# A decoder layer whose last stage adds finished tiles to the output in DRAM by DMA

## The chip, the cores and the metric

The kernel runs on one core of a Trainium2 chip. A core has a matrix engine (TensorE, PE in the profile, with PEld for its weight loads), VectorE (DVE), ScalarE (ACT), GpSimd (POOL) and SyncE (SP), which here only issues DMAs. Each engine takes its instructions in order; semaphores hold an instruction until what it needs is done. Matmul results land in PSUM, which has banks of 512 float32 per partition; everything else on chip lies in SBUF. Sixteen DMA engines move data between SBUF and DRAM. SP's DMAs go through the queue that the profile calls q1, GpSimd's through q0; only GpSimd's can add to their destination instead of overwriting it.

The metric is the device time of one execution in microseconds, smaller is better.

## The reference

One decoder layer over a sequence of 1024 tokens with 1024 features, all in float32:

```
x = x + 0.5 * swiglu(rms_norm(x) ; ffn1)            # 1024 -> 2816 -> 1024
h = rms_norm(x) @ w_in                              # q, k, v and gates of two attentions
x = x + (sig(g_fox) * (fox @ w_bf) + sig(g_sb) * (stick @ w_bs)) @ w_out
x = x + 0.5 * swiglu(rms_norm(x) ; ffn2)
x = x + sigmoid(rms_norm(x) @ w_ple_gate) * (p @ w_ple_proj)
```

`fox` is causal softmax attention with forget gates, `stick` is stick-breaking attention. The change touches the first line, small parts of the others, and the last line.

## The kernel before, in words

**Exact products from rounded operands.** TensorE is fed in the faster type float32r. So each operand is split into a high half (a copy rounded to float32r, on ScalarE) and a low half (the rest, a subtraction on VectorE, sometimes on GpSimd); a product is high x high + high x low + low x high. `split` does this for a weight tile, `high` and `low` for the activations. A product over 512 features is 12 matmuls of 128x128 weights by 512 columns.

**Seven products instead of eight.** `make_up` computes a 1024 x 256 block of weights against 1024 x 1024 activations, cut 2 x 2, by a Strassen scheme: block `n` has products `(n, m)`, m = 1 to 7, whose operands are sums of quarters. On the activation side these sums are `B[m]`, made once per stage by the `combo_...` functions on VectorE and ScalarE, quarter by quarter (`j` = 0 to 3). On the weight side `sums`, `third_sum` and `last_sum` form them from the raw tiles, in place. Product `(n, m)` adds into an open PSUM bank: 1, 6, 7, 4 share one (`b`), 5 and 3 another (`d`), 2 has its own (`a`). `evict(n, m, ps)` takes what is finished out of PSUM and combines it in the tiles `E[n]`.

**The order is written by hand.** `up_order` gives the list of products. The loop of `ffn` (and that of `end` in the last stage) does for step s: the product and its `evict`, then `begin(s)`, which issues the pieces of the activation sums that are due, then `prep` of the product four steps on (`LA = 4`), which splits its weights and, at certain products, forms the block's sums or issues the load of block n + 2. Within `ffn` each engine runs in the order of the program (`manual_schedule`); the attention between the two FFNs is placed by a scheduler. Buffers rotate by tag: a load whose tag is full waits until the tile that it replaces has been read, and since SP is in order everything behind it on SP waits too. In the first FFN the raw weights of the up projection lie in the tags KH and KL, where the activations' working tiles lie too.

In the first FFN (`rows` is true there) steps 8 to 12 are (1,3), (3,1), (1,4), (2,4), (3,2). Product (1,4) is the first to read `B[4]`, which `begin` makes in steps 4 to 8: a difference (`combo_d`), then high and low half (`combo_e`, `L651` and `L655`).

**The head.** `first_entry` loads the rows of x, takes their norms (`rows_stat`: a square with a row sum on ScalarE, plus epsilon, to the power of minus one half on GpSimd), multiplies (`rows_mul`, VectorE), turns them by TensorE (`turn`) and splits them (`rows_high`, `rows_low`). `busy` runs idle matmuls at the start. `plain` is the product of block 0, which is not done by the scheme.

**Norms between the stages.** While the last down products of a stage (`make_down`, steps i = 0 to 6 of four tiles t each) still run, `up_step` already takes the next norm: the squares, a sum over partitions by four thin matmuls (`norm_sum`, L194), the root (`norm_pow`: L199 on ScalarE, L200 on GpSimd), and a turn of the result into a row by TensorE (`norm_row`, L206). In i = 5 the sum stands after t = 1 and the row after t = 2. This holds for the entry of the second FFN and of the last stage; the entry of the attention has its own code.

**The last stage** (`ple_start`). The down products of the second FFN leave x in SBUF; `finished` also stores it to DRAM, into `x_end` (`xe`). The stage has four blocks. `E[n][i]` (i = 0, 1) is a tile of 128 x 2 x 512, the sigmoid of the gate for one 128-row part of the output, its halves called h0 and h1. The table `AT` says what happens at the end of each step: `fetch` loads a tile of the projection `p_proj` (or, with `True`, of the residual x) by SP; `finish` multiplies `E` by the projection (L1722) and then either lets GpSimd issue a DMA that adds the residual from `x_end` into the SBUF tile (L1724) or, `late`, adds a fetched residual on VectorE (L1726); `store` writes the tile to the output by SP (L1730). The last product, (3,4), runs in two halves of 256 columns, in one PSUM bank, with a sigmoid (L1784) after each. Steps 10 to 18 are (3,1), (2,4), (3,2), (3,6), (3,5), (3,7), (2,3), (3,3), (3,4).

## Time and profile before

| | us |
|---|---|
| median of 3 runs | 2250.58 (2249.4 to 2251.67) |
| the profiled execution | 2251.57 |
| its span, first to last instruction | 2249.8 |
| busy: TensorE, VectorE, ScalarE, GpSimd | 2215.0, 1513.7, 1004.5, 817.1 |
| mean granted TensorE clock | 0.998 of full |

A row of the timeline reads: start and duration in us, engine, source line, operation, output <- inputs by tile tag, partitions x elements, how many instructions the row joins, and in brackets how long the engine stood idle before the first and what released it. SPq and POOLq rows are DMA issues. Consecutive instructions of one kind are joined, also where they overlap, so starts are the better measure of a pace. A row of the waits reads: engine, tile, line, `<-` what it waited for, then us in total, times, and the longest. A row of windows gives the stretch and its length, busy us and count for PE, PEld, DVE, ACT, POOL, the granted clock, the share of the 16 DMA engines, and GB/s. A DMA queue's row gives packets, MB and its share of the 16 engines in the window asked for; a DMA issue's row the size and the time to landing.

### The profile page before, as it was taken

Reading aid. Unit: us, or ns where it says so; the run is one execution under the profiler, and the core shown is the slowest. Engines: PE = TensorE matmul, PEld = TensorE weight load, DVE = VectorE, ACT = ScalarE, POOL = GpSimd, SP = SyncE. Lnnn points to the kernel's source line nnn. Section 1 sums busy time; section 2 is a strip of 40 time slices with the busy share of each in tenths; the row PEclk is TensorE's granted clock in tenths of the full one; section 3 lists DMA queues with packets and bytes.
Section 4 is the critical chain, followed back from the end, with each engine's and each line's share of the span. In section 5 each row is a group of like instructions: output and inputs, shape, how many; then the busy total and the mean of one; then the engine's idle time right before and its main releaser. Section 6 shows DMA issues by size and latency. Waiting matters only on the chain. (4 is left out here: it accounts for less than half of the span.)

```text
span 2249.8 us, 30560 instructions
## 1 busy us (share of the span) xinstructions
PE 2215.0 (98%) x11226; PEld 1880.4 (84%) x11226; DVE 1513.7 (67%) x2366; ACT 1004.5 (45%) x1805; POOL 817.1 (36%) x787
## 2 busy tenths in 40 slices
PE   9999999999999999999999999999999999999997
PEld 7788888888888899999898888888888888888886
DVE  8755545598888324666678885789655545778887
ACT  6333333433455435555566663255333333434453
POOL 1343534210021336556566664420544353200111
PEclk9999999999999999999999999999999999999999
DMA  3332323394322334333324366741423232655327
GB/s 132 101 129 80 131 80 131 114 345 171 115 94 98 128 108 127 85 104 89 82 57 100 108 206 218 245 155 52 141 85 126 80 132 80 243 206 192 123 84 224
DMA packets 196184, 298.04 MB, mean 132 GB/s; under 512 B 28730, under 2 KB 108858, under 8 KB 196035
## 3 DMA queue, kind: packets, MB, share of 16 engines
q1 hardware_dynamic: 195312, 293.47, 39.4%
q0 software_dynamic: 720, 2.62, 0.6%
q8 instruction: 88, 1.44, 0.3%
q14 instruction: 62, 0.50, 0.1%
q10 hardware_dynamic: 2, 0.00, 0.0%
HBM read 196.14 MB, written 83.13 MB: 124 GB/s over the span
## 5 line engine op out<-in xcount | busy, mean ns | idle before, releaser
L509 PE MATMUL ps<-H,H 128*128 128x512 f32 x2184 | 497.2, 390 | 0.0
L509 PEld LDWEIGHTS ps<-H,H 128*128 128x128 f32 x2184 | 409.7, 188 | 84.7
L619 PE MATMUL ps<-H,WL 128*128 128x512 f32 x1176 | 278.0, 389 | 0.0
L619 PEld LDWEIGHTS ps<-H,WL 128*128 128x128 f32 x1176 | 220.8, 188 | 45.8
L185 POOL TENSOR_TENSOR PT<-PT,PT 128x512 f32<-128x512 f32 x27 | 34.9, 1293 | 400.7 <-ACT PT L182 399.8
L619 PE MATMUL ps<-H,Q 128*128 128x512 f32 x612 | 145.6, 389 | 0.0
L517 DVE SCALAR_TENSOR_TENSOR X<-ps,X 128x512 f32<-128x512 f32 x168 | 110.3, 686 | 47.6 <-PE ps L509 47.3
L619 PE MATMUL ps<-X,WL 128*128 128x512 f32 (+1 forms) x576 | 135.9, 385 | 0.5 <-ACT KH L1784 0.5
L619 PEld LDWEIGHTS ps<-H,Q 128*128 128x128 f32 x612 | 114.9, 188 | 23.8
L619 PE MATMUL ps<-H,PT 128*128 128x512 f32 x528 | 125.8, 390 | 0.0
L619 PEld LDWEIGHTS ps<-X,WL 128*128 128x128 f32 x576 | 106.7, 188 | 22.2 <-ACT KH L1784 0.7
L139 POOL TENSOR_TENSOR WL<-RAW,WH 128x512 fp32r<-128x512 f32 (+1 forms) x84 | 98.4, 1192 | 67.9 <-ACT WH L129 38.7
L1223 DVE TENSOR_TENSOR PT<-ps,PT 128x512 fp32r<-128x512 f32 (+1 forms) x160 | 100.1, 627 | 30.7 <-ACT PT L1217 29.8
L900 PE MATMUL ps<-WH,H 128*128 128x256 f32 x768 | 116.2, 288 | 0.8 <-ACT RN L965 0.8
L619 PEld LDWEIGHTS ps<-H,PT 128*128 128x128 f32 x528 | 99.0, 188 | 20.5
L908 PE MATMUL ps<-H,WH 128*128 128x512 f32 x384 | 115.1, 407 | 0.0
L1241 PE MATMUL ps<-PT,X 128*128 128x256 f32 (+1 forms) x640 | 102.5, 286 | 6.4 <-DVE PT L1223 5.4
L1217 ACT CAST PT<-ps 128x512 fp32r<-128x512 f32 (+1 forms) x160 | 87.0, 549 | 42.2 <-PE ps L1215 40.8
L1241 PEld LDWEIGHTS ps<-PT,X 128*128 128x128 f32 x640 | 90.3, 190 | 17.0 <-DVE PT L1223 10.5
L900 PEld LDWEIGHTS ps<-WH,H 128*128 128x128 f32 x768 | 101.5, 190 | 2.7 <-ACT RN L965 1.2
L412 POOL TENSOR_TENSOR PT<-GF,RN 128x512 f32<-128x512 f32 x20 | 33.6, 1680 | 189.8 <-DVE GF L808 189.8
L1169 POOL TENSOR_TENSOR T<-T,l 128x128 f32<-128x128 f32 (+3 forms) x64 | 73.2, 1147 | 71.9 <-DVE l L1168 69.8
(457 smaller groups left out, 4792.2 us busy)
## 6 DMA issues: line engine op xcount, KB each, us to landing
hidden<-PT SPq DMA_DIRECT2D x40, 512.0 KB, 2.7
WH<-in_ffn_w_gate_dram SPq DMA_DIRECT2D x38, 512.0 KB, 4.8
Q<-hidden SPq DMA_DIRECT2D x24, 512.0 KB, 6.2
hidden<-RN SPq DMA_DIRECT2D x22, 512.0 KB, 2.6
KH<-in_ffn_w_up_dram SPq DMA_DIRECT2D x20, 512.0 KB, 6.2
KL<-in_ffn_w_up_dram SPq DMA_DIRECT2D x20, 512.0 KB, 6.9
T<-in_ffn_w_down_dram SPq DMA_DIRECT2D x20, 512.0 KB, 6.2
GF<-hidden SPq DMA_DIRECT2D x14, 512.0 KB, 8.0
```

What stands on the lines that cost most here:

```text
L139: ins = eng_lo.tensor_sub(lo[part], raw[part], f(hi[part]))
L185: add = lambda eng: eng.tensor_add(N["acc"], N["acc"], d)
L412: eng.tensor_add(s12[:, 0, :], g1[:, 1, :], g2[:, 1, :])
L509: pe(nc.tensor.matmul(groups[g][t][:], wt[:, b, k, t * P:(t + 1) * P], act[:, a, k, :], start=(fresh and n == 0), stop=(i in (6, 1, 4) and ...
L517: nc.vector.scalar_tensor_tensor(xs, groups[g][t][:], scale, xs, ALU.mult, ALU.add)
L619: pe(nc.tensor.matmul(ps[:, cols], hl[:, a, k, :], right(B[m], b, k)[:, cols], start=(first and i == 0), stop=(final and i == 11), skip_gr ...
L900: pe(nc.tensor.matmul(ps[:, :n], hT[t // 4](a, k)[:, (t % 4) * P:(t % 4 + 1) * P], w[k // 4][b][:, k % 4, :n], start=(i == 0), stop=(i == ...
L908: pe(nc.tensor.matmul(ps[:], w[a][:, k, :], hT[half](b, k), start=(i == 0), stop=(i == 23)))
L1169: nc.gpsimd.tensor_mul(T[:, :n], T[:, :n], l[:].broadcast_to([P, n]))
L1217: high = nc.scalar.copy(pt[:, 0, :width], ps[:, :width])
L1223: ins = nc.vector.tensor_sub(pt[:, 1, :width], ps[:, :width], f(pt[:, 0, :width]))
L1241: pe(nc.tensor.matmul(o, lh, r, start=(kpair == c and i == 0), stop=(kpair == 0 and i == 3)))
```

## The change

1. **Last stage.** `xe` is no longer a tensor of its own but a view of the kernel's output: x is stored there at the end of the second FFN, and residuals are fetched from there. A finished tile is added to the output in DRAM: GpSimd's DMA has the output as destination and the SBUF tile as source. `store` goes. Tiles that are late are, as before, added on VectorE and then written. Products (2,3) and (2,4) change places (steps 11 and 16). By DMA now go both tiles of blocks 0 and 1, (2,0), half h1 of (2,1) and h0 of (3,0); late are h0 of (2,1), h1 of (3,0), and (3,1). The fetches are set anew.
2. **First FFN's order.** Steps 9 to 16 become (3,1), (3,2), (1,4), (2,4), (2,3), (3,6), (3,5), (3,7). The preparations of (1,4) and (3,2) keep the order that they had (`ahead`). The sums of block 3 move from the preparation of (3,2) to that of (3,6), GpSimd's `last_sum` with them.
3. **`begin`.** The first `combo_s` goes from step 1 to step 0, `third_sum(2)` from step 3 to step 2, in all three stages of this kind.
4. **Norms.** In i = 5 the sum is taken after t = 0 instead of t = 1.
5. **Head.** The DMA of the norm's gain is issued ahead of the activation that loads the table; epsilon is added by GpSimd for three of the first four row tiles; `F.prep(0, 2)` goes ahead of `rows_stat(N[1], 0)` and `rows_low(N[0], 3)`; `F.prep(2, 1)` goes ahead of `F.l(0)`.
6. The scaling of `gqk`, a column of 64 numbers for the attention, goes from VectorE to GpSimd.

```
         elif i == 5:
-            if t == 1:
+            if t == 0:
                 norm_sum(N[0], bank("pt"))
...
         if rows:
-            seqn.insert(-1, (3, 1))
-        for n in range(3, nm_ - 1):
-            seqn += [(n, 1)][rows and n == 3:] + [(n - 1, 4), (n, 2), (n - 1, 3), (n, 6), (n, 5), (n, 7)]
+            seqn[-1:] = [(3, 1), (3, 2), (1, 4), (2, 4), (2, 3), (3, 6), (3, 5), (3, 7)]
+        for n in range(4 if rows else 3, nm_ - 1):
+            seqn += [(n, 1), (n - 1, 4), (n, 2), (n - 1, 3), (n, 6), (n, 5), (n, 7)]
...
-            if m == (2 if n == 3 else 1) and n > 2:
+            late = n == 3 and rows()
+            if m == (6 if late else 2 if n == 3 else 1) and n > 2:
                 sums(n, nc.vector if n == 3 else nc.gpsimd)
+                if late:
+                    last_sum(n)
...
-            if m == 2 and n > 2:
+            if m == 2 and n > 2 and not late:
                 last_sum(n)
...
             if s == 0:
                 sums(2, nc.vector, True)
+                combo_s(0, 7)
             elif s == 1:
-                for q in range(4):
+                for q in range(1, 4):
                     combo_s(q, 7)
             elif s == 2:
                 last_sum(1, nc.vector)
+                third_sum(2, nc.vector)
             elif s == 3:
-                third_sum(2, nc.vector)
                 load(3)
...
+        ahead = list(seqn)
+        if "w" in tags:
+            ahead[10], ahead[11] = ahead[11], ahead[10]
...
-                    U.prep(*seqn[s + LA])
+                    U.prep(*ahead[s + LA])
...
         load_x(0)
-        nc.scalar.activation(stat([P, 1], "ss")[:], mhalf[:, 0:1], AF.Silu)
         gB = slot("PT", [P, D])
         nc.scalar.dma_start(gB[0:1, :], ffn1_norm[0].unsqueeze(0))
+        nc.scalar.activation(stat([P, 1], "ss")[:], mhalf[:, 0:1], AF.Silu)
...
-            rows_stat(N[0], t, ("PT", "WL", "WL", "PT")[t], True)
+            rows_stat(N[0], t, ("PT", "WL", "WL", "PT")[t], t == 0)
...
         rows_low(N[0], 2)
+        F.prep(0, 2)
         rows_stat(N[1], 0, "Y")
         rows_low(N[0], 3)
-        F.prep(0, 2)
...
         F.t(1)
+        F.prep(2, 1)
         F.l(0)
         ps = F.product(1, 2)
         F.t(2)
-        F.prep(2, 1)
...
-    nc.vector.tensor_scalar(gqk[0:HD, :], gqk[0:HD, :], HD ** -0.5, None, ALU.mult)
+    nc.gpsimd.tensor_scalar(gqk[0:HD, :], gqk[0:HD, :], HD ** -0.5, None, ALU.mult)
...
-    xe = dp.tile([KD, P, S], F32, name="x_end")
+    xe = out[0].rearrange("(k p) n -> k p n", p=P)
...
             e = E[n][i][:, h, cols]
+            dst = xe[2 * n + i].rearrange("p (h n) -> p h n", h=2)[:, h, cols]
             nc.vector.tensor_mul(e, e, T[n, i][:, h, cols])
             if add_in_dma:
-                nc.gpsimd.dma_start(e, xe[2 * n + i].rearrange("p (h n) -> p h n", h=2)[:, h, cols], accum_op=ALU.add)
+                nc.gpsimd.dma_start(dst, e, accum_op=ALU.add)
             else:
                 nc.vector.tensor_add(e, e, T[n, i, "x"][:, h, cols])
-                store(n, i, h, cols)
+                nc.sync.dma_start(dst, e)
...
-        AT = {6: [(fetch, 1, 0, "Q"), (fetch, 1, 1, "WH")], 7: [(finish, 0, 0)], 8: [(finish, 0, 1), (fetch, 3, 0, "Q", True), (fetch, 2, 1, "T")],
-              9: [(fetch, 3, 0, "T"), (fetch, 3, 1, "KL", True)], 10: [(finish, 1, 0)], 11: [(finish, 1, 1), (fetch, 3, 1, "Q"), (store, 0, 0)], 12: [(store, 0, 1)],
-              13: [(finish, 2, 1), (fetch, 2, 0, "RAW"), (fetch, 2, 0, "RAW", True)], 14: [(finish, 3, 0, h0, *late), (store, 1, 0)], 15: [(store, 1, 1)],
-              16: [(finish, 3, 1, h1, *late)], 17: [(store, 2, 1), (finish, 2, 0, slice(0, 2), *late), (finish, 3, 0, h1, *late)]}
+        AT = {6: [(fetch, 1, 0, "Q"), (fetch, 1, 1, "WH")], 7: [(finish, 0, 0)], 8: [(finish, 0, 1), (fetch, 2, 0, "T"), (fetch, 3, 0, "Q")],
+              9: [(fetch, 2, 1, "T"), (fetch, 2, 1, "RAW", True), (fetch, 3, 1, "KL")], 10: [(finish, 1, 0), (fetch, 3, 0, "Q", True)], 11: [(finish, 1, 1), (fetch, 3, 1, "WH", True), (finish, 2, 1, h1)],
+              13: [(finish, 2, 0)], 14: [(finish, 3, 0, h0)], 16: [(finish, 3, 1, h1, *late), (finish, 2, 1, h0, *late)], 17: [(finish, 3, 0, h1, *late)]}
...
             seqn = up_order(4)
+            seqn[11], seqn[16] = seqn[16], seqn[11]
```

2 lines of the change are left out of this document (removed).

## The prediction, made before the changed kernel was run

> **What bounds the kernel now.** I read the page's busy shares first, then the matrix engine's waits, then the stretches of the timeline around each wait, and last the DMA view of the closing 40 us.
>
> ```profile
> PE 2215.0 (98%) x11226; PEld 1880.4 (84%) x11226; DVE 1513.7 (67%) x2366; ACT 1004.5 (45%) x1805; POOL 817.1 (36%) x787
> PE ps L206 <- POOL rs L200: 4.5, 3, 1.6
> PE ps L619 <- DVE X L655: 2.2, 1, 2.2
> PE ps L563 <- DVE WL L106: 1.3, 1, 1.3
> ```
>
> PE is busy in 98% of the 2249.8 us, so no edit outside PE's order can gain more than PE's holes: 34.8 us in all. The change adds and removes no matmul. What it can move are the waits above (two of the three at L206 lie where it touches) and the end, where PE has stopped and the kernel has not:
>
> ```profile
> 2234.69 0.69 DVE L1753 TENSOR_TENSOR KH<-KH,ps 128x512 f32<-128x512 f32 x1 [0.70 <-PE ps L619]
> 2236.56 1.70 PE L619 MATMUL ps<-X,WL 128*128 128x256 f32 x12 [0.47 <-ACT KH L1784]
> 2240.32 1.23 DVE L1722 TENSOR_TENSOR Y<-Y,RAW 128x1024 f32<-128x1024 f32 x1 [4.94 <-DMA RAW<-p_proj]
> 2245.30 0.42 DVE L1726 TENSOR_TENSOR KH<-KH,KL 128x256 f32<-128x256 f32 x1
> 2240.00:2245.00 5.00, 0.00 (x0) 0.00 (x0) 4.57 (x7) 0.00 (x0) 0.00 (x0) 0.83 1.03 418
> ```
>
> The last matmul ends at 2238.26, VectorE waits until 2240.32 for a fetched tile, ends at 2245.72, and the span ends 4.1 us later. In the windows row the last two columns are the share of the 16 DMA engines and GB/s: the engines are full (1.03) to the end.
>
> **Part 1, the head (small orders).**
>
> ```profile
> 14.44 3.67 DVE L287 TENSOR_TENSOR H<-ps,H 128x512 fp32r<-128x512 f32 x6
> 18.76 3.02 PE L563 MATMUL ps<-H,WL 128*128 128x512 f32 x12 [1.34 <-DVE WL L106]
> 23.88 0.69 DVE L655 TENSOR_TENSOR X<-Q,X 128x512 fp32r<-128x512 f32 x1 [0.33 <-ACT X L651]
> 32.06 0.69 DVE L655 TENSOR_TENSOR X<-KL,X 128x512 fp32r<-128x512 f32 x1 [0.54 <-ACT X L651]
> ```
>
> `F.prep(0, 2)` goes ahead of one square on ScalarE and of the last two of six subtractions on VectorE. Its low half now follows four of them: 14.44 + 4 x 0.61 = 16.88, done at 17.56, so the 12 matmuls start at about 17.6, not 18.76: PE is 1.15 us earlier. The two delayed subtractions end at 18.8; the last eight matmuls, which read them, start at 18.5 with the half that is ready. ScalarE then copies earlier what PE turns, and VectorE's two waits on it (0.33 + 0.54 = 0.87) go. None of this is a gain by itself: VectorE sets what PE finds 50 us later, so it counts in part 2.
>
> At nothing I put: the gain's DMA issue ahead of the table load (its reader stands behind ten warming matmuls); the three epsilon additions moved from ScalarE to GpSimd (VectorE's row multiplications, back to back until the row at 14.44, set the pace; without that cover, 0.2 us each); the scaling of `gqk` moved to GpSimd, idle there (0.13 off VectorE; if its DMA is late, GpSimd's next root is held and the row that VectorE multiplies by it); and `F.prep(2, 1)` one place earlier: VectorE's wait of 1.21 for its high half stays, at another place.
>
> **Part 2, the first FFN's products.**
>
> ```profile
> 56.15 0.69 DVE L106 TENSOR_TENSOR WL<-RAW,WL 128x512 fp32r<-128x512 f32 x1 [0.69 <-ACT WL L105]
> 63.00 0.69 DVE L106 TENSOR_TENSOR WL<-WH,WL 128x512 fp32r<-128x512 f32 x1 [0.74 <-ACT WL L105]
> 68.73 2.88 PE L619 MATMUL ps<-T,WL 128*128 128x512 f32 x12
> 71.45 0.84 PE L619 MATMUL ps<-H,WH 128*128 128x512 f32 x3
> 72.04 0.37 SPq L544 DMA_DIRECT2D KL<-in_ffn_w_up_dram  x1
> 74.88 1.19 PE L619 MATMUL ps<-X,Q 128*128 128x512 f32 x4 [0.54 <-ACT X L651]
> 75.06 0.68 DVE L792 TENSOR_TENSOR Y<-Y,ps 128x512 f32<-128x512 f32 x1
> 75.79 0.62 ACT L105 CAST WL<-KL 128x512 fp32r<-128x512 f32 x1 [0.96 <-DMA KL<-in_ffn_w_up_dram]
> 77.52 0.68 DVE L655 TENSOR_TENSOR X<-KL,X 128x512 fp32r<-128x512 f32 x1
> 78.26 3.00 PE L619 MATMUL ps<-X,Q 128*128 128x512 f32 x8 [2.18 <-DVE X L655]
> 84.57 2.89 PE L619 MATMUL ps<-H,WL 128*128 128x512 f32 x12
> 80.00:90.00 10.00, 10.00 (x39) 8.09 (x39) 5.98 (x8) 1.80 (x4) 9.11 (x6) 0.87 0.57 213
> ```
>
> A product takes 71.45 - 68.73 = 2.72. After (3,1) come (1,4), which stalls twice, and (2,4): 10.40 us from 74.17 to 84.57 where two products take 5.44. The loss, 4.96, is more than the waits of 2.7, because the granted clock falls (0.87 in the window's row). Here the Trainium skill, "TensorE: Matmul & The Clock Gate", section on the HAM clock gate, says that about 3.4 us of idling throttle the clock; this trace shows a drop after holes of 0.7 and 2.2 with four matmuls between. By its rule the drop would not be there, and the loss to be won would be about 3.
>
> Now (3,2) runs ahead of (1,4), so (1,4) finds its operand's last part (77.52) in time. What is late next is (3,2) itself: its weights go into the KL buffer that the low half of (1,4) frees; SP issues at 72.04, ScalarE copies at 75.79, 3.75 later. The preparation of (1,4) still stands ahead of that of (3,2), so this chain stays. VectorE reaches it sooner: one `combo_s` fills the wait of 0.69 at 56.15 (0.60 of work), and `third_sum` one step earlier leaves 0.15 of the 0.74 at 63.00; with part 1's 0.87, about 2.1. Then SP issues at 69.9, the copy runs at 73.65 and ends at 74.3; PE, there at 73.0, waits 1.25. Queued behind that copy on ScalarE and VectorE are the operand parts of (1,4): VectorE does the low half of (3,2), 74.35 to 75.0, then the three steps that now run from 75.06 to 77.52, and the last part (0.68) to 78.1; (1,4), which begins at 77.0, needs that by its eighth matmul, 78.6. Moved too: the sums of block 3 (three on VectorE, one on GpSimd) go two preparations later, where VectorE has idle time (busy 5.98 of 10 us above). The three products end at 74.3 + 8.16 = 82.5, against 84.57 + 2.72 = 87.3: **4.8**. Without part 1's share on VectorE it is 4.0. Lower bound: the DMA is no earlier, the copy ends at 76.45, and a hole of 2.3 lowers the clock as now: 2.7 less 1.8, **0.9**. Upper: no hole, 4.96 + 1.15 = **6.1**. I take **4.5**, nearest to the replayed order.
>
> **Part 3, the norm's sum one step earlier, twice.**
>
> ```profile
> 2133.61 0.69 DVE L185 TENSOR_TENSOR PT<-PT,PT 128x512 f32<-128x512 f32 x1 [0.83 <-ACT PT L182]
> 2136.34 1.99 ACT L105 CAST H<-Q 128x1024 fp32r<-128x1024 f32 x2
> 2137.33 0.95 PE L194 MATMUL ps<-ones,PT 128*128 128x1 f32 x8
> 2141.33 0.15 ACT L199 ACTIVATE rs<-ps 128x4 f32<-128x4 f32 x1
> 2141.56 1.02 POOL L200 TENSOR_TENSOR rs<-rs,mhalf 128x4 f32<-128x4 f32 x1 [9.08 <-ACT rs L199]
> 2142.64 0.65 PE L206 MATMUL ps<-identf,rs 128*128 128x128 f32 x4 [1.47 <-POOL rs L200]
> 1507.09 0.65 PE L206 MATMUL ps<-identf,rs 128*128 128x128 f32 x4 [1.60 <-POOL rs L200]
> ```
>
> The sum moves to 2137.33 - 2.72 = 2134.6; its addend is done at 2134.3, 0.3 in hand. ScalarE is free at 2138.3, where the copy L199 no longer queues behind a square of the next half; the root is ready at 2139.6; PE comes for it at 2141.2. Both waits go: 1.47 + 1.60, **3.0** (2 if the sum has to wait).
>
> **Part 4, the last stage.** Six units of half a megabyte (five whole, two halves) are accumulated into the output instead of five into SBUF; the five stores after them and their waits on SP go. VectorE loses one long and one half addition net of what it gains; each leaves the path at the end.
>
> ```profile
> 2217.59 0.47 SPq L1717 DMA_DIRECT2D KL<-x_end  x1
> 2228.57 0.34 SPq L1730 DMA_DIRECT2D out_dram<-RN  x1
> 2228.96 0.49 SPq L1717 DMA_DIRECT2D RAW<-p_proj  x1
> q0 software_dynamic: 148, 0.54, 67.7%
> q1 hardware_dynamic: 150, 0.54, 36.2%
> q1 hardware_dynamic: 543, 1.67, 103.4%
> q0 software_dynamic: 720, 2.62, 15.7%
> out_dram<-GF SPq DMA_DIRECT2D x1, 512.0 KB, 12.1
> ```
>
> Before, the fetch that VectorE awaits at 2240.32 was issued only at 2228.96, behind a store that waited for an accumulation. That hold goes. If nothing replaced it, VectorE would follow PE: last sigmoid 2238.67, two steps to 2239.5, **6.2** earlier than 2245.72.
>
> But the DMA engines are the next bound. Of the q rows, the first two are 2228 to 2232, the third 2240 to 2244, the fourth 2160 to 2250. Alone, q1 (SP) moves 1.67 MB in 4.14 engine-us: 1.3 per half megabyte. An accumulation takes 15.7% of 90 us for five: 2.82 each. While both queues are full they moved the same bytes (0.54 MB in 4 us), about 3.7 us for half a megabyte on each. This is the rule of the Trainium skill, "DMA: Bandwidth & Descriptors", section on queues, rings and completion order, that an engine takes turns between queues packet by packet; the trace agrees (148 and 150 packets). The same page fits 2.0 us + bytes / 436 GB/s to one DMA, 3.2 for half a megabyte; by that the tail would have the 6.2, but the row for a store shows 12.1.
>
> In the new order SP has five fetches from about 2218 (the row at 2217.59 stands at that place): the projection of (2,1), its residual, the projection of (3,1), the residuals of (3,0) and (3,1). At 3.7 each the fifth lands at 2218 + 18.5 + 0.7 = 2237.2, while GpSimd's accumulations (six units at some 3.8) keep their queue full. Step 16 adds that fifth tile on VectorE. **Behind this new wait** are: the pair of (2,1) (2238.6), the addition L1753 of product 17 (done 2239.9), ScalarE's sigmoid and the first half of the last product (2240.9), PE's second half, which waits for that (row 2236.56), its sigmoid and two steps: 7 us, so 2244.2. Stores meet emptier queues, 0.4. Taken: **2.0** earlier. Bounds: 6.2, and below nothing as an accumulation into DRAM is not in this trace: if it holds an engine f times as long as one into SBUF, the fetch takes 3.7 (1.30 + 2.82 f) / 4.12, and the tail is 1.3 later than now at f = 1.25, 4.4 at 1.5, 10.8 at 2. I take f = 1: both kinds read two streams and write one, and plain stores ran at 418 GB/s, as fast as anything here.
>
> **Sum**: 4.5 + 3.0 + 2.0 = 9.5 against this execution's own 2251.57 (its span 2249.8 and 1.8 around it). The three runs' median, 2250.58, is 1.0 lower, so 2241.1.
>
> **Rivals.** (A) *Accumulating into DRAM is dearer.* For it: not one such packet in the trace, and everything in step 16 hangs on one fetch. At f about 1.75 it eats the 7.5 of the other parts, and from f = 2.1 the kernel is **slower**, 2255 or more. Against: the equal streams. Between 1.4 and 2.1: 2246 to 2255. (B) *The tail is freed whole*, because the two queues share better than 3.7: 13.7 off, 2237. For it: VectorE idles 4.94 before 2240.32. Against: the packet counts. (C) *The weights' DMA paces part 2*: 0.9 instead of 4.5, so 2244.7. For it: SP's issue hangs on VectorE, which is full there. (D) *The output orders its own DMAs*: fetches of the residual wait for accumulations into other rows of the same tensor; the fifth fetch then lands near 2241, 2245. Against: none of SP's waits here is one store to the output on another.
>
> **How the numbers follow.** Forecast 0.45; A 0.12 in the middle and 0.10 slower; B 0.12; C 0.13; D 0.08. A measurement of this kernel tells 0.2%, 4.5 us, from no change: faster ends at 2246.1, slower begins at 2255.1. Faster: forecast, B, C and D's nearer half, 0.76; same 0.14; slower 0.10. The range goes from B's 2236 to 2250, inside A's middle.
>
> **What would show it.** Part 1: the wait at L563 of 1.3 falls to 0.7 or less. Part 2: no wait at L655; one of about 1.2 on ScalarE's copy; granted clock 1.00 from 70 to 90. Part 3: two of three waits at L206 gone. Part 4: no store behind an accumulation on SP; VectorE's longest wait in the last 20 us is on the residual of (3,1), ended near 2227 by the new clock; q0 and q1 with equal packets until then. It is wrong if an accumulation of half a megabyte takes over 5 us of engine time, or if SP waits on one.

## The result, and the profile after

The changed kernel takes 2239.59 us in the median of five runs (2238.65 to 2240.01), against 2250.58 before: 11.0 us less, ratio 0.995 with a 95% interval of 0.9936 to 0.9965. Measured a second time beside another version it gave 2240.6, ratio 0.9948 (0.9936 to 0.9961). The prediction was 2241.1, with faster as the likeliest sign. Its parts were less right than its sum, so the two profiled executions (2251.57 and 2238.65, spans 2249.8 and 2236.9) are compared by stretches between marks on PE: *a*, the second half of the first plain product; *b*, product (3,6) of the first FFN; *c*, the first product of the attention's entry; *d*, the down products that follow the attention; *e*, the first plain product of the second FFN; *f*, the first product behind the last stage's norm row (L206); *g*, VectorE's end; *h*, the span's end.

| stretch | before | after | gain | forecast |
|---|---|---|---|---|
| start to a (head) | 18.76 | 18.91 | -0.15 | in the next row |
| a to b (first FFN's order) | 71.26 | 67.70 | 3.56 | 4.5 for both rows |
| b to c (a norm) | 568.87 | 567.18 | 1.69 | 0 |
| c to d (attention) | 782.92 | 782.44 | 0.48 | 0 |
| d to e (a norm) | 79.38 | 77.58 | 1.80 | 1.6 |
| e to f (a norm) | 621.85 | 620.17 | 1.68 | 1.5 |
| f to g (last stage to VectorE's end) | 102.68 | 99.81 | 2.87 | 1.5 |
| g to h (last transfers) | 4.08 | 3.11 | 0.97 | 0.4 |
| sum | 2249.8 | 2236.9 | 12.9 | 9.5 |

The head after the change, from the timeline (the last row is mark a; the view was cut at 20 us, so it joins fewer matmuls):

```profile
1.32 4.45 PE L253 MATMUL ps<-T 128*128 128x512 bf16 x10 [1.32 <-DVE T L249]
5.70 2.12 PE L239 MATMUL ps<-PT,T 1*128 1x512 f32 x4
11.29 1.46 POOL L265 TENSOR_TENSOR rt<-ss,mhalf 128x1 f32<-128x1 f32 x1
12.79 1.28 DVE L268 SCALAR_TENSOR_TENSOR PT<-X,rt,PT 128x1024 f32<-128x1024 f32 x1 [0.46 <-POOL rt L265]
18.91 1.43 PE L563 MATMUL ps<-H,WL 128*128 128x512 f32 x5 [0.38 <-DVE WL L106]
```

The wait at L563 fell from 1.34 to 0.38, as the reordering was to do. But PE came to the first half of that product at 15.52, where before it came at 14.18, and the gain was gone. The first four rows say why: ten warming matmuls took 4.45, and a row multiplication waited 0.46 for GpSimd's root, an instruction on one column that took 1.46. Both are looked at below.

The first FFN after, from the timeline:

```profile
71.06 0.37 SPq L544 DMA_DIRECT2D KL<-in_ffn_w_up_dram  x1
74.77 0.62 ACT L105 CAST PT<-KL 128x512 fp32r<-128x512 f32 x1 [1.96 <-DMA KL<-in_ffn_w_up_dram]
75.44 3.02 PE L622 MATMUL ps<-H,PT 128*128 128x512 f32 x12 [0.92 <-ACT PT L105]
78.30 3.04 PE L622 MATMUL ps<-X,Q 128*128 128x512 f32 x12
86.61 2.88 PE L622 MATMUL ps<-H,WL 128*128 128x512 f32 x12
```

and its windows row for 80 to 90 (the third column from the end is the granted clock):

```profile
80.00:90.00 10.00, 10.00 (x45) 8.26 (x44) 8.49 (x10) 3.60 (x6) 7.48 (x5) 1.00 0.56 205
```

Product (3,2), at 75.44, waits 0.92 for ScalarE's copy, which waits for the DMA that SP issued at 71.06; (1,4), at 78.30, waits for nothing, and the clock is 1.00 where it was 0.87.

The last stage's norm, the first and the fifth of SP's last fetches, and the end, from the timeline:

```profile
2127.23 0.95 PE L194 MATMUL ps<-ones,PT 128*128 128x1 f32 x8
2133.62 0.60 PE L206 MATMUL ps<-identf,rs 128*128 128x128 f32 x4
...
2207.53 0.32 SPq L1724 DMA_DIRECT2D T<-p_proj  x1
2213.89 0.33 SPq L1724 DMA_DIRECT2D WH<-out_dram  x1
2226.79 0.69 DVE L1734 TENSOR_TENSOR KH<-KH,WH 128x512 f32<-128x512 f32 x1 [3.13 <-DMA WH<-out_dram]
2230.40 2.05 PE L622 MATMUL ps<-X,WL 128*128 128x256 f32 x12 [2.60 <-ACT KH L1789]
2233.36 0.43 DVE L1734 TENSOR_TENSOR KH<-KH,WH 128x256 f32<-128x256 f32 x1
```

The DMA queues, in 2219 to 2223 (two rows) and q0 in 2150 to 2237:

```profile
q0 software_dynamic: 145, 0.53, 66.1%
q1 hardware_dynamic: 151, 0.55, 36.7%
...
q0 software_dynamic: 1008, 3.15, 18.7%
```

L206 waits for nothing. VectorE's longest wait at the end is the forecast one, 3.13 on the residual of (3,1); the chain behind it takes 2233.79 - 2226.79 = 7.0. While both queues are full they move equal packets. Six accumulations take 18.7% of 87 us, 2.71 each, against 2.82 into SBUF.

### The profile page after: what moved, and what is told of

It reads as the page before. It is cut to its first block, busy times and chain, and to the rows that moved or that the text cites. A ratio compares the mean times of both kernels' runs of the same rounds, so it can differ in the third digit from the quotient of the medians.

```text
span 2236.9 us, 30553 instructions
## 1 busy us (share of the span) xinstructions
PE 2213.2 (99%) x11226; PEld 1879.6 (84%) x11226; DVE 1515.7 (68%) x2365; ACT 1004.8 (45%) x1802; POOL 823.8 (37%) x793
## 3 DMA queue, kind: packets, MB, share of 16 engines
q0 software_dynamic: 1008, 3.15, 0.7%
## 4 chain that ended last, share of the span: by engine, by line
PE 88%; DVE 7%; ACT 2%; issue 1%; DMA 1%; POOL 0%; SPq 0%; DVEq 0%; ACTq 0%; POOLq 0%
PE ps L622 39%; PE ps L509 22%; PE ps L907 8%; PE ps L915 5%; PE ps L1510 4%; PE ps L1248 3%; PE ps L563 2%; PE ps L1222 2%; PE ps L1164 1%; PE ps L1163 1%; PE ps L1069 1%; DVE PT L1230 1%; DVE RN L1126 1%; DVE GF L1126 1%; DMA WH<-out_dram 1%
## 5 line engine op out<-in xcount | busy, mean ns | idle before, releaser
L1230 DVE TENSOR_TENSOR PT<-ps,PT 128x512 fp32r<-128x512 f32 (+1 forms) x160 | 99.8, 626 | 29.6 <-ACT PT L1224 28.9
```

The lines of the kernel that those rows point to most:

```text
L1230: ins = nc.vector.tensor_sub(pt[:, 1, :width], ps[:, :width], f(pt[:, 0, :width]))
```

## The experiments

Times of single executions are read by the stretches of the table above, because the head and the attention scatter from run to run and would hide an edit. All profiled executions together:

| label | to a | a-b | b-c | c-d | d-e | e-f | f-g | g-h | span |
|---|---|---|---|---|---|---|---|---|---|
| before | 18.76 | 71.26 | 568.87 | 782.92 | 79.38 | 621.85 | 102.68 | 4.08 | 2249.8 |
| after | 18.91 | 67.70 | 567.18 | 782.44 | 77.58 | 620.17 | 99.81 | 3.11 | 2236.9 |
| after_again | 21.15 | 67.62 | 567.17 | 783.03 | 77.58 | 620.17 | 99.52 | 3.16 | 2239.4 |
| head_gain_back | 19.51 | 67.71 | 567.18 | 782.63 | 78.28 | 620.16 | 99.67 | 3.16 | 2238.3 |
| head_both_back | 18.31 | 68.25 | 567.18 | 782.64 | 77.57 | 620.17 | 100.63 | 3.15 | 2237.9 |
| eps_back | 18.21 | 68.27 | 567.17 | 782.62 | 77.58 | 620.17 | 100.57 | 3.11 | 2237.7 |
| order_back | 19.80 | 69.04 | 567.18 | 782.55 | 78.30 | 620.16 | 99.66 | 3.11 | 2239.8 |
| begin_back | 19.68 | 68.77 | 567.18 | 783.16 | 77.58 | 620.17 | 101.38 | 3.18 | 2241.1 |
| norm_back | 18.51 | 68.37 | 568.88 | 783.12 | 79.38 | 621.85 | 99.61 | 3.18 | 2242.9 |
| tail_old | 19.48 | 67.84 | 567.18 | 782.88 | 78.53 | 620.17 | 101.13 | 4.29 | 2241.5 |
| tail_swap | 19.68 | 67.81 | 567.17 | 782.54 | 77.58 | 620.16 | 98.21 | 6.85 | 2240.0 |
| accum_plain | 19.60 | 68.40 | 567.18 | 783.20 | 77.58 | 620.16 | 97.38 | 3.10 | 2236.6 |
| three | 21.44 | 66.22 | 567.18 | 782.88 | 77.58 | 620.17 | 99.27 | 3.16 | 2237.9 |
| best2 | 18.40 | 66.85 | 567.18 | 783.29 | 78.32 | 620.16 | 98.20 | 3.10 | 2235.5 |

Where TensorE ran the two halves of the plain product without a break (after_again, begin_back, three), mark a is the start of the thirteenth of the 24 matmuls, which the joined row of the timeline doesn't show. In begin_back it comes late because PE ran at half clock from 14.21 to 17.63, behind two waits of 0.77 at the row multiplications.

### The head: three runs

head_gain_back puts the gain's DMA behind the activation again:

```
         load_x(0)
+        nc.scalar.activation(stat([P, 1], "ss")[:], mhalf[:, 0:1], AF.Silu)
         gB = slot("PT", [P, D])
         nc.scalar.dma_start(gB[0:1, :], ffn1_norm[0].unsqueeze(0))
-        nc.scalar.activation(stat([P, 1], "ss")[:], mhalf[:, 0:1], AF.Silu)
```

head_both_back does that and takes epsilon back to ScalarE; eps_back does only the latter:

```
-            rows_stat(N[0], t, ("PT", "WL", "WL", "PT")[t], t == 0)
+            rows_stat(N[0], t, ("PT", "WL", "WL", "PT")[t], True)
```

> The changed kernel with the gain's DMA issued behind the table-loading activation again, as before the change. Theory 'order': the DMA that now goes out first, beside the first row loads and ahead of the table load, lands later, and this moved L239 from 4.95 to 5.70 us and the first row multiplication from 7.76 to 8.65. Then both go back, L239 to about 4.95, and the first matmul of the plain product starts at about 14.6 instead of 15.52; the span falls by 0.5 to 0.9. Rival 'luck': the landing of this one-row DMA varies between executions whatever its order; then L239 stays near 5.7, or stands anywhere, and nothing follows the edit.

> As the kernel with the gain's DMA put back, and epsilon added on ScalarE again for all four row tiles. Theory 'GpSimd in the chain': the two operations on GpSimd per row tile (L264, L265) hold the fourth row multiplication for 0.46 us; with one of them back on ScalarE that wait goes, and the plain product starts another 0.4 us earlier, at about 14.2, as before the change. Rival: ScalarE's 0.2 us per tile comes back into the chain and eats it; no difference from the kernel with the gain alone put back.

> The changed kernel with one thing undone: the epsilon addition of the first four row roots is on ScalarE again, not on GpSimd; the gain's DMA stays ahead of the table load. Theory P (the one-column instructions of GpSimd are stretched while VectorE multiplies a row, and the addition is a second instruction exposed to that): VectorE's waits at the row multiplications on GpSimd's root, 0.46 + 0.77 = 1.23 in five of the eight heads with the addition on GpSimd (none to 1.54 in the others), fall to 0.5 at most, the last two subtractions start at 18.2 to 18.5 instead of 18.4 to 19.7, and since everything behind that is paced by PE, the time falls by about 1 us: 2238.4 as a median where the changed kernel had 2239.6. Rival (the head's scatter comes only from when the input's rows land): the waits stay near 1.2 wherever the third row tile lands late, and the median stays at 2239.6 give or take 0.3.

Measured: 2240.06 and 2239.65 us in single runs; eps_back 2239.87 in the median (2238.92 to 2242.06), ratio 0.9946 (0.9934 to 0.9958). So neither edit shows in the time. The traces show what scatters. First PE's rate, in the warming matmuls of two executions, eps_back and after_again (the changed kernel itself, below):

```profile
1.32 3.80 PE L253 MATMUL ps<-T 128*128 128x512 bf16 x10 [1.32 <-DVE T L249]
6.97 2.33 PE L253 MATMUL ps<-T 128*128 128x512 bf16 x10
```

```profile
1.32 4.45 PE L253 MATMUL ps<-T 128*128 128x512 bf16 x10 [1.32 <-DVE T L249]
5.70 3.78 PE L239 MATMUL ps<-PT,T 1*128 1x512 f32 x4
9.41 4.29 PE L253 MATMUL ps<-T 128*128 128x512 bf16 x10
```

The same ten matmuls take 2.33 at the full rate and 4.45 at about half. Over the fourteen executions the first ten took 3.62 to 4.45. The trace's record of the granted clock begins with the change to the full rate: at 3.97 us in the best (begin_back), at 6.02 in the changed kernel's first profile, at 13.41 and 14.09 in two (after_again and three). Ahead of the record a windows row reads 1.00 and doesn't show the half rate. L239, the gain's spread over the partitions, starts when the ten are done, 4.88 to 5.70, whichever way round the gain's DMA was issued; so that order costs and gains nothing, as was predicted, and the 0.75 that the changed kernel's profile lost there was PE's rate. The Trainium skill, "TensorE: Matmul & The Clock Gate", section on the HAM clock gate, has PE at half rate until a free-running window of about 3.4 us has been busy, with a start that varies between runs; the variation agrees. The two late executions ran matmuls without a break from 1.3 to 13 us at half rate, and agree only if L239's matmuls, which have one row of weights, don't count as busy. Cut the time before the change into steps of 3.41 us (the length of a half-rate stretch, see the last section). The step that ends at the change holds 2.65 us or more of warming matmuls in all fourteen executions, and no earlier step holds over 2.53. No run tests this alone.

Second, GpSimd. order_back's head (its edit comes later), with epsilon on GpSimd:

```profile
11.62 1.28 DVE L268 SCALAR_TENSOR_TENSOR WL<-X,rt,PT 128x1024 f32<-128x1024 f32 x1 [0.46 <-POOL rt L265]
11.66 1.31 POOL L264 TENSOR_SCALAR ss<-ss 128x1 f32<-128x1 f32 x1
13.06 0.57 POOL L265 TENSOR_TENSOR rt<-ss,mhalf 128x1 f32<-128x1 f32 x1
13.66 1.28 DVE L268 SCALAR_TENSOR_TENSOR PT<-X,rt,PT 128x1024 f32<-128x1024 f32 x1 [0.77 <-POOL rt L265]
```

The addition of epsilon to one column, 0.22 elsewhere, lasts 1.31, until the row multiplication that began just ahead of it on VectorE is over; then comes the root, and the next row multiplication has waited 0.77. The Trainium skill, "SBUF — State Buffer", section "SBUF: two separate sides", says that a VectorE instruction with two operands in SBUF and a GpSimd instruction that reads SBUF exclude each other for the whole length of the one that began first; this trace agrees. With epsilon on GpSimd the waits at L268 sum to 1.23 in five executions, 1.54 in one, 0.46 in one and none in norm_back and after_again; with it on ScalarE they are at most 0.45. So theory P holds for VectorE: the prediction's "at nothing" was 0.8 to 1.1 there in most executions. For the kernel's time it doesn't: where mark a comes at 18.2 to 18.5 (head_both_back, eps_back, norm_back), a-b is 68.25 to 68.37 where the other executions with the same order have 67.62 to 67.84 (accum_plain 68.40), so half of it is lost again, and the medians can't tell the rest from the scatter. The same stretching loses it, further on. From eps_back, the eighth row multiplication and PE behind it:

```profile
25.88 1.28 DVE L268 SCALAR_TENSOR_TENSOR PT<-X,rt,PT 128x1024 f32<-128x1024 f32 x1 [0.46 <-POOL rt L265]
32.29 3.96 PE L622 MATMUL ps<-H,PT 128*128 128x512 f32 x16 [0.22 <-DVE PT L106]
```

These two waits stand in the three executions and in order_back, accum_plain and best2, and in no other. They cost about 0.5 from a to the start of (3,1).

### The first FFN: two runs

order_back undoes part 2 of the change (product order, `ahead`, the place of block 3's sums) and keeps `begin`; begin_back undoes part 3 and keeps the order:

```
-            seqn[-1:] = [(3, 1), (3, 2), (1, 4), (2, 4), (2, 3), (3, 6), (3, 5), (3, 7)]
-        for n in range(4 if rows else 3, nm_ - 1):
-            seqn += [(n, 1), (n - 1, 4), (n, 2), (n - 1, 3), (n, 6), (n, 5), (n, 7)]
+            seqn.insert(-1, (3, 1))
+        for n in range(3, nm_ - 1):
+            seqn += [(n, 1)][rows and n == 3:] + [(n - 1, 4), (n, 2), (n - 1, 3), (n, 6), (n, 5), (n, 7)]
```

```
             if s == 0:
                 sums(2, nc.vector, True)
-                combo_s(0, 7)
             elif s == 1:
-                for q in range(1, 4):
+                for q in range(4):
                     combo_s(q, 7)
             elif s == 2:
                 last_sum(1, nc.vector)
-                third_sum(2, nc.vector)
             elif s == 3:
+                third_sum(2, nc.vector)
                 load(3)
```

> The changed kernel with the first FFN's order of products and preparations as before (block 3's sums back at the preparation of (3,2)); the earlier pieces in steps 0 and 2 stay. Theory 'the order makes room': (1,4) waits again for the last quarter of its operand, less than before because VectorE is 1 to 1.3 us earlier: a wait of about 1 to 2 at L658 and the loss by a lower clock with it; the three products up to (3,2) end 2 to 3.5 us later. Rival 'VectorE's earliness did it': no wait over 0.5 there and less than 1 us lost.

> The changed kernel with the first combo_s in step 1 and third_sum in step 3 again, the new order kept. Theory 'VectorE paces the buffer that the weights' DMA waits for': SP issues that DMA 1.0 to 1.3 us later (at about 72.2), the copy of its tile runs at about 75.9, and the matrix engine's wait before (3,2) grows from 0.92 to about 2.1; if the clock falls as in the kernel before, some 1.5 more. Rival: the landing does not follow the issue, and the wait stays near 1.

Measured: 2241.55 and 2242.77 us; a-b is 69.04 and 68.77, where the executions with both edits have 67.62 to 68.40 and before, with neither, 71.26. From the start of (3,1) to (3,6), which leaves out the head's 0.5, it is 15.80 and 16.20, with both edits 14.97 to 15.19, and before 18.57. PE's rows around the stall, order_back and then begin_back with its DMA issue:

```profile
75.76 1.07 PE L622 MATMUL ps<-X,Q 128*128 128x512 f32 x4
78.73 2.11 PE L622 MATMUL ps<-X,Q 128*128 128x512 f32 x8 [1.91 <-DVE X L658]
80.68 2.88 PE L622 MATMUL ps<-X,PT 128*128 128x512 f32 x12
```

```profile
72.84 0.37 SPq L544 DMA_DIRECT2D KL<-in_ffn_w_up_dram  x1
76.56 0.62 ACT L105 CAST PT<-KL 128x512 fp32r<-128x512 f32 x1 [1.98 <-DMA KL<-in_ffn_w_up_dram]
77.23 3.03 PE L622 MATMUL ps<-H,PT 128*128 128x512 f32 x12 [2.10 <-ACT PT L105]
```

With the old order (1,4) still stalls in its middle, 1.91 instead of 2.18, but the products behind it keep their 2.72: the clock doesn't fall here. So of the 2.77 between before and order_back, 0.81 are shorter holes (0.54 + 2.18 against 1.91) and 1.7 is the clock, which before had at half for 3.42 us behind its hole, from 79.22 to 82.64. That leaves 0.25 for PE's second start. With the new order and the old `begin`, (3,2) waits 2.10 for the copy instead of 0.9 to 1.1: VectorE gives the buffer KL free later, and the fetch behind it takes the same 3.7. Apart from the clock's 1.7, which neither run lost, `begin` alone is worth 1.1, the order alone 0.7, and both together 1.7 to 1.9.

### The norms

```
         elif i == 5:
-            if t == 0:
+            if t == 1:
                 norm_sum(N[0], bank("pt"))
```

> The changed kernel with the norm's sum after t = 1 again. The prediction counted two places and 3.0 us. Theory 'three places, and the restart of the weight loads counts': all three waits at L206 return, each 1.5 of matrix time and 1.7 from product to product, and the span grows by 5.0 to 5.2. Rival 'as predicted': two waits matter, 3.0 to 3.5.

Measured 2244.6 us, and the waits on the root are back:

```profile
PE ps L206 <- POOL rs L200: 4.6, 3, 1.6
```

b-c, d-e and e-f are longer by 1.70, 1.80 and 1.68, the three numbers that the change had won. The price of a place is more than its wait (1.48, 1.60, 1.47): PE also starts anew behind it. The other stretches stay within their scatter. The edit has a price too: in four of the twelve executions that have it (head_gain_back, order_back, tail_old, best2) the sum comes a little before its last addend:

```profile
1493.51 1.05 PE L194 MATMUL ps<-ones,PT 128*128 128x1 f32 x8 [0.51 <-DVE PT L185]
```

That is best2, in the entry of the second FFN; d-e is 78.28 to 78.53 in these four instead of 77.58, so 0.7 to 0.95 of the 1.80 is lost again. At the entry of the last stage, where the prediction had worked out a margin of 0.3, the sum never waits.

### The last stage: three runs

tail_old has the last stage as before in the otherwise changed kernel:

```
-    xe = out[0].rearrange("(k p) n -> k p n", p=P)
+    xe = dp.tile([KD, P, S], F32, name="x_end")
...
-            seqn[11], seqn[16] = seqn[16], seqn[11]
```

with `finish`, `store` and `AT` as they were. So it undoes the destination, the order and the fetches together; no run separates them. accum_plain writes where the kernel adds:

```
             if add_in_dma:
-                nc.gpsimd.dma_start(dst, e, accum_op=ALU.add)
+                nc.gpsimd.dma_start(dst, e)
```

tail_swap exchanges the second and the fifth of SP's fetches and ends (2,1) in step 17 (the row that moves its `finish` is left out here):

```
-              9: [(fetch, 2, 1, "T"), (fetch, 2, 1, "RAW", True), (fetch, 3, 1, "KL")], 10: [(finish, 1, 0), (fetch, 3, 0, "Q", True)], 11: [(finish, 1, 1), (fetch, 3, 1, "WH", True), (finish, 2, 1, h1)],
+              9: [(fetch, 2, 1, "T"), (fetch, 3, 1, "RAW", True), (fetch, 3, 1, "KL")], 10: [(finish, 1, 0), (fetch, 3, 0, "Q", True)], 11: [(finish, 1, 1), (fetch, 2, 1, "WH", True), (finish, 2, 1, h1)],
```

> The changed kernel with the last stage as before the change: accumulation into SBUF, stores by SP, the old products' order and fetches. The ledger of the two traces puts 3.9 us on this stage (2.9 until VectorE's end, 1.0 behind it). Theory 'the ledger holds': the span grows by 3.4 to 4.4, and VectorE again waits some 5 us for a fetch that SP issued behind a store. Rival 'the stage gains only by the earlier start': less than 2.

> The changed kernel with GpSimd's accumulating DMAs of the last stage turned into plain ones of the same tiles to the same place: the residual is left out in six units of the output, to see what the accumulation itself costs. Theory 'turns by packet, and an accumulating packet holds an engine twice as long': GpSimd's queue takes about 1.3 to 1.5 engine-us for half a megabyte instead of 2.7, SP's fetches move at about 2.5 instead of 3.7 us each, the residual of (3,1) lands 5 us earlier, near 2221.5, the wait in step 16 goes, and the span falls by about 3. Rival 'GpSimd's queue or SP's issue is the limit': the fetch still lands after 2225 and the span moves by less than 1.

> The changed kernel with two fetches of the last stage exchanged: the residual of (3,1) is fetched second and that of (2,1) fifth, and the late half of (2,1) is finished after (3,0) in step 17 instead of in step 16. The same bytes in the same queues. Theory 'one late fetch in VectorE's order': the residual of (3,1) lands some 8 us earlier, step 16 waits for nothing, the second half of the last product no longer waits 2.6 us, and VectorE ends 2.5 to 3.3 us earlier in relation to the last product, the span 2 to 3.3 shorter. Rival 'the queues are the bound': whatever lands fifth, at about 2226.8, sets the end, which moves by less than 1.

Measured: 2243.16, 2238.35 and 2241.74 us. From f to the end the new stage takes 102.7 to 102.9 (after, after_again, head_gain_back, norm_back, order_back), or 103.7 to 104.6 where its last matmuls ran at half clock (head_both_back, eps_back, begin_back; see the last section). The old one takes 105.42 in tail_old and 106.76 before. So the stage is worth 2.5 to 4.1, and tail_old's 2.5 to 2.7 against undisturbed executions lies between the theory's 3.4 and the rival's 2. VectorE waits there for a projection that SP issued behind a store, as before, but 3.55 instead of 4.94. accum_plain takes 100.48. The queue of GpSimd in it over 2150 to 2237, and VectorE's addition of the last residual:

```profile
q0 software_dynamic: 880, 3.15, 8.9%
2225.90 0.69 DVE L1734 TENSOR_TENSOR KH<-KH,WH 128x512 f32<-128x512 f32 x1
```

Six plain writes take 7.7 engine-us, 1.29 each; adding costs as much again and a little, 2.71. With that off the engines SP's second, third and fourth fetch land 2.4 and 2.5 apart, where they landed 3.8 and 3.8 apart in the changed kernel, the last one is in time, VectorE doesn't wait, and the stage gains 2.2 to 2.4. The single run's 2238.35 hides this, as its head, its first FFN and its attention are each 0.7 to 0.8 longer than in the changed kernel's first profile.

tail_swap's fetch of (3,1) is in time too, and VectorE ends 98.21 behind f instead of 99.5 to 99.8. But the span then ends 6.85 later instead of 3.1, because of this row on GpSimd:

```profile
2227.21 1.75 POOL L1732 DMA_DIRECT2D out_dram<-Y  x2 [9.73 <-DMA WH<-out_dram]
```

The fetch of (2,1)'s residual now stands ahead of GpSimd's accumulation into its half h1, and reads those rows; the accumulation must wait until the fetch, fifth in its queue, has read them, and two more stand behind it on GpSimd. So the output does order two DMAs here, but this isn't rival D of the prediction: there a fetch was to wait for accumulations into other rows, here an accumulation waits for a fetch of the same rows.

### Two versions, and the changed kernel again

three and best2 take epsilon back to ScalarE and prepare (1,4) ahead of (3,1) in the first FFN:

```
-            ahead[10], ahead[11] = ahead[11], ahead[10]
+            ahead[9:12] = [(1, 4), (3, 1), (3, 2)]
```

three also fetches only the used half of the residuals of (2,1) and (3,0). best2 exchanges the fetches as tail_swap does, but fetches only half h0 of (2,1):

```
-        def fetch(n, i, tag, x=False):
+        def fetch(n, i, tag, x=False, h=slice(0, 2)):
...
-            nc.sync.dma_start(t[:], (xe if x else pd)[2 * n + i].rearrange("p (h n) -> p h n", h=2))
+            nc.sync.dma_start(t[:, h], (xe if x else pd)[2 * n + i].rearrange("p (h n) -> p h n", h=2)[:, h])
```

> The same, with two edits more, each read in its own stretch. (1) In the first feed-forward stage the operand of product (1,4) is prepared one place earlier, ahead of (3,1)'s, so that the buffer KL comes free and its DMA is issued one preparation earlier. Theory: PE's wait before (3,2), 0.9 to 1.1 in the heads so far, goes, and the stretch from the first plain product's second half to (3,6), 67.7 to 67.8, becomes 66.7 to 66.9. Rival: the operand of (3,1), now one place later, is late instead, and a wait of 0.3 to 1.5 stands before (3,1). (2) In the last stage the two fetches of the residual of which only one half is used, (2,1) and (3,0), fetch that half: 0.5 MB less on SP's queue. Theory (SP's fifth fetch is paced by both queues' bytes, 3.7 us for half a megabyte): the residual of (3,1) lands 2 to 3.5 us earlier, VectorE's wait of 3.13 on it falls under 1, and the stretch from the first product behind the last norm's row to VectorE's end, 99.6 to 99.8, becomes 97.4 to 98.2 (accumulations made plain gave 97.4), with the span's end 3.1 behind as now. Rival (the accumulations, not SP's fetches, end last): that stretch shortens but the end stays 102.8 to 102.9 behind the same product. Sum by the theories: 2239.6 - 1.0 - 1.0 - 2.0 = 2235.6 as a median.

> The changed kernel with three edits, each read in its own stretch: epsilon of the first four roots on ScalarE; the operand of (1,4) prepared ahead of (3,1)'s; and in the last stage the residual of (3,1) fetched second and that of (2,1) fifth, of the latter only the half that VectorE adds, so that GpSimd's accumulation into the other half doesn't touch the fetched rows. Theory O (the order of SP's fetches, in turns of packets, sets VectorE's wait, and in the run that swapped whole fetches GpSimd's accumulations were late only because the fetch of (2,1) read rows that they write): no wait on a fetched residual over 0.5, GpSimd issues its fifth accumulation within 18 of the first as in the changed kernel, VectorE ends 98.2 behind the first product after the last norm's row (99.8 before), and the span's end 101.2 to 101.6 behind it (102.9 before). Rival: the half fetch is waited for in its turn, or the accumulations end last in any order, and the end stays 102.6 or later. In part 2 no wait before (3,2) or (3,1), 66.3 to 66.9 from the plain product's second half to (3,6). Median by the theories: 2239.7 less 1.2 for part 2 less 1.5 for the tail, 2237.0; 2238.5 by the rival.

> The changed kernel itself once more, beside the last one on the same chip. If the scatter of its head comes from when TensorE reaches its full rate, and from GpSimd's instructions stretched under VectorE's row multiplications, then ten warming matmuls take between 3.6 and 4.5, the waits at the row multiplications are 0.46 to 1.54 in sum, and the stretches behind the head repeat: 67.7 to 67.8 from the plain product's second half to (3,6), 102.8 to 102.9 from the first product after the last norm's row to the end. If these stretches move by over 0.3 instead, differences under 1 us between single executions say nothing of the edits. Median 2239.6.

Measured: three 2236.82 us in the median (2234.72 to 2239.58), ratio 0.993 (0.9918 to 0.9942); best2 2237.25 (2235.65 to 2240.07), ratio 0.9934 (0.9921 to 0.9948); after_again, on the chip of best2, 2240.6. In both versions no product from (3,1) to (3,6) waits. From the one to the other it is 13.60, five times 2.72, where it was 14.97 to 15.19: freeing KL one preparation earlier is worth 1.4 to 1.6. a-b is 66.22 and 66.85.

In three, however, VectorE still waits 2.70 on the residual of (3,1), and f-g is 99.27, almost as it was. Half a megabyte less ahead of it brought the landing forward by 0.4, not by 2 to 3.5. The queues while it waited in its turn, 2218.47 to 2222.47:

```profile
q0 software_dynamic: 167, 0.61, 77.0%
q1 hardware_dynamic: 180, 0.43, 30.2%
```

Again about as many packets on both, but SP's are now 2.4 KB instead of 3.6: the half fetches have shorter packets, not fewer, and the turns go by packets. That is what "DMA: Bandwidth & Descriptors" of the Trainium skill says in its section on queues, rings and completion order, and what the prediction had quoted for equal sizes; the expectation of three had forgotten it.

best2 moves the turn instead of the bytes, and theory O holds on all counts:

```profile
2223.97 0.69 DVE L1734 TENSOR_TENSOR KH<-KH,RAW 128x512 f32<-128x512 f32 x1
2231.98 0.42 DVE L1734 TENSOR_TENSOR KH<-KH,RAW 128x256 f32<-128x256 f32 x1
```

No wait on a fetch, VectorE ends 98.20 behind f, the span 101.30. By the medians best2 is 3.4 us faster than the changed kernel beside it, about 15 faster than before. after_again repeats a-b, b-c, d-e and e-f within 0.1 and f to h within 0.25; its head (21.15, a slow start of PE) and its attention are what made it 2.5 longer than the first profile.

## Why the prediction was right, and where its steps were not

**The sum.** 9.5 was forecast, 12.9 is the difference of the two profiles, 11.0 that of the medians. Of the 3.4 between forecast and profiles the norms give 2.2, the last stage 1.8, the attention 0.5; head and first FFN together take 1.1 back. The attention's 0.5 is chance: the same code takes 782.44 to 783.29 over thirteen executions, with before in the middle.

**Part 1.** The mechanism held, the wait at L563 fell below 0.7, and the gain's order did cost nothing. The step that failed put the epsilon additions at nothing ("without that cover, 0.2 us each"): the cover, VectorE's row multiplications, is what stretches GpSimd's instruction. Beside it the 1.15 were an edit's worth in a stretch that itself scatters between 18.2 and 21.4. No run undoes the two `F.prep` edits or the one of `gqk`, so their worth is argued and not shown.

**Part 2.** (3,2) was late next, on ScalarE's copy, with no wait left at the activation part, as replayed. Mis-sized was how much sooner VectorE reaches the buffer: SP issued 0.98 earlier, not 2.1. The two moves in `begin` gave 1.0 of their 1.2 (in begin_back SP issues that much later behind mark a), and part 1's 0.87 didn't arrive: the subtraction that stood at 56.15 before came at 56.38. The hole was 0.92 instead of 1.25, as PE came later. Rival C's mechanism, the weights' DMA, is thus the one that remained; best2 and three remove it. The bounds held, but 1.7 of the loss that the prediction set out to win was the clock's, and that hangs on where a hole falls (last section): order_back's products behind a hole of 1.91 lose nothing.

**Part 3.** The step "twice" was wrong, and with it the description of the kernel: the entry of the attention also goes through `up_step`, so all three waits at L206 went, 5.17 instead of 3.0. The third row stood in the list of waits (4.5, three times) and was not traced to its place.

**Part 4.** The pace was right: from the first to the landing of the fifth of SP's fetches it is 2226.79 - 2207.53 = 19.3, against 19.2 forecast; so were the 7 us behind it, and f = 1 (2.71 against 2.80 in tail_old). The step that failed is "from about 2218": by the clock of before, SP began at 2216.6, 1.4 earlier, and that is the missing 1.4 of the stretch to VectorE's end. The last transfers ended 0.97 sooner instead of 0.4. Rival A falls with that f: an accumulation costs in DRAM what it cost in SBUF, by accum_plain a good two plain writes. Rival B did not come: the stage gained 3.8 of its 6.2. best2, which accumulates as much, gains 5.5 (101.30 against 106.76), so most of what was missing hung on the order of the fetches. D appeared in no run.

**The chances.** With the nearer half of D at 0.04, faster adds up to 0.74, not 0.76.

## What to carry to other kernels

A DMA that waits behind another queue is paced by packets, so move it forward in its queue or give it fewer packets; shorter ones save next to nothing. When an edit's place is named by one line in the waits, trace every occurrence to its place before counting. Compare single executions by stretches between marks on the bounding engine: here the head scattered by 3 us, the last stage by 2 and the attention by 1 and hid edits of 1 to 2, while the stretches without holes (b to c, e to f) repeated within 0.02. Look up the granted clock of a stretch before its loss is put down to an edit.

## What the runs showed of the hardware

The last product's second half stands behind a hole in which PE waits 2.2 to 2.8 for its bank. It took 1.69 or 1.70 in three executions, 1.80 to 2.05 in three, and 2.93 in three (head_both_back, eps_back, begin_back), and f-g is 0.9 to 1.9 longer in these than in the first three. From eps_back, the two halves:

```profile
2226.27 1.59 PE L622 MATMUL ps<-X,WL 128*128 128x256 f32 x12
2230.33 2.93 PE L622 MATMUL ps<-X,WL 128*128 128x256 f32 x12 [2.47 <-ACT KH L1789]
```

Behind a hole of 0.47 (before, tail_old, tail_swap, accum_plain, best2) it was 1.69 or 1.70 each time. So here a hole of 2.2 to 2.8 may cost the rate or may not, in the same program. The granted clock tells the cases apart. Where PE got its rate back it had been at half for 3.41 or 3.42 us: in eps_back from 2229.82 to 2233.23, in before from 79.22 to 82.64, in begin_back from 14.21 to 17.63. These are two steps of that length in eps_back and then two in after_again, whose second half took 1.70 (PE's busy time stands third in a row, the clock third from the end):

```profile
2226.41:2229.82 3.41, 1.45 (x13) 1.24 (x11) 2.58 (x4) 0.45 (x1) 0.00 (x0) 1.00 1.06 210
2229.82:2233.23 3.41, 2.90 (x12) 2.63 (x12) 2.14 (x4) 0.45 (x2) 0.00 (x0) 0.50 0.64 232
2228.66:2232.07 3.41, 1.96 (x15) 1.68 (x13) 2.44 (x4) 0.00 (x0) 0.14 (x1) 1.00 1.07 210
2232.07:2235.49 3.42, 1.70 (x12) 1.49 (x12) 2.43 (x6) 1.28 (x3) 0.00 (x0) 1.00 0.69 222
```

In the six executions with a longer second half PE was busy for 1.1 to 1.5 us of the step that ends where the clock falls, in before's first FFN for 1.2, in begin_back's head for 1.6. In the three without, and at begin_back's wait of 2.10 in the first FFN, no step that the hole touches has under 1.7. So in these stretches the clock fell behind a step with 1.6 us of work or less and held behind one with 1.7 or more. Where in the steps a hole falls decides, and that is luck. The Trainium skill, "TensorE: Matmul & The Clock Gate", section on the HAM clock gate, puts the bound at an idle window of about 3.4 us; these runs show the loss behind shorter holes.
